# Stick-breaking attention: from cumulative sums by matmul to a sigmoid, a scan along the keys and DMA transposes, emitted by a stream scheduler

## The chip, the cores and the metric

One Trainium2 chip, all 8 cores, each with one of the 8 sequences of the batch; no core needs another. The metric is the device time of the slowest core in microseconds (us). Executions fall in a fast state or in a slower one, in which the cores of one die or of both are granted a lower TensorE clock (in the change's run of 3783.9 us 0.81 to 0.82 on cores 0 to 3, 0.92 to 0.93 on the others); only fast executions are compared here, and a range of fast runs is given where it matters. Ratios are the mean time of one kernel's fast runs over that of the other's fast runs of the same rounds on the same chip, with a 95% interval, so they are not quite the ratio of the medians quoted.

Names: PE is TensorE (matmul), PEld its weight load, DVE VectorE, ACT ScalarE, POOL GpSimd, SP SyncE, which here only starts DMAs. "L954" is line 954 of the kernel in question; experiments that add lines shift these numbers by a few.

## The reference, cut to what matters

Two layers on a (2048, 2048) sequence: an mLSTM layer with 8 heads, then a stick-breaking layer with 16 heads of width 128. Each ends with an output projection and a layer norm. The second layer's attention:

```python
# [cut] q, k, v: [B, H, S, 128], swept in blocks of 128 queries over the causal prefix
z = jnp.einsum("bhtd,bhsd->bhts", qb, kp) * scale
mask = jnp.arange(t1)[None, :] < (t0 + jnp.arange(QBLOCK))[:, None]
log_1mb = jnp.where(mask, jax.nn.log_sigmoid(-z), 0.0)
between = lax.cumsum(log_1mb, axis=3, reverse=True) - log_1mb   # sum over s<j<t
a = jnp.where(mask, jnp.exp(jax.nn.log_sigmoid(z) + between), 0.0)
outs.append(jnp.einsum("bhts,bhsd->bhtd", a, vp))
# [cut] y = (att * silu(z_gate)) @ w_out; x = LayerNorm(alpha * x + y)
```

With r(s) the product of sigmoid(-z) over the keys from s to the query, a weight is a(s) = r(s+1) - r(s). That is what the change uses: one sigmoid, one running product, one subtraction of neighbours.

## The kernel before

A small layer records every operation with the tiles it reads and writes, and places the semaphore waits, each as an instruction of its own:

```python
def _wait(self, e, dep):
    # [cut] nothing to do if e has already seen this value
    self.seen[e][sn] = v
    self.eng[e].wait_ge(self.semobj[sn], v)

def op(self, e, fn, R=(), W=(), inc=True):
    R, W = self._norm(R, W)
    self._deps(e, R, W)          # _wait for each writer of R, each writer and reader of W
    ins = fn()
    # [cut] then_inc, bookkeeping
```

Stick-breaking, keys on partitions. Per step (512 queries by 128 keys) three ACT passes and four matmuls; the projections of the next head are a generator of which each step pulls two portions of four matmuls:

```python
# s_front(k)
kb.op("pe", lambda: P_.matmul(PS[zb][:, fs], lhsT=KT[...], rhs=QT[:, qs], ...))      # QK
kb.op("act", lambda: A_.activation(out=E[i][:, fs], in_=PS[zb][:, fs], func=AF.Exp, scale=scale), ...)
kb.op("act", lambda: A_.activation(out=SP[i][:, fs], in_=E[i][:, fs], func=AF.Ln, bias=1.0, scale=1.0), ...)
# [cut] masks on POOL on the diagonal
# s_utri(k), s_tri(k): the cumulative sum along keys as two triangular matmuls
kb.op("pe", lambda: P_.matmul(PS[2][:, fs], lhsT=NUTRI[:], rhs=SP[i][:, fs], ...), ...)
kb.op("pe", lambda: P_.matmul(PS[2][:, fs], lhsT=NTRI[:], rhs=SP[i][:, fs], ...), ...)
kb.op("act", lambda: A_.activation(out=X[xi][:, fs], in_=PS[2][:, fs], func=AF.Exp), ...)
kb.op("dve", lambda: V.tensor_tensor(out=AT[ai][:, fs], in0=E[i][:, fs], in1=X[xi][:, fs], op=ALU.mult), ...)
# s_av(k)
kb.op("pe", lambda: P_.matmul(PS[3][:, fs], lhsT=VV[:, sg, :], rhs=AT[ai][:, fs], ...), ...)
# the sweep
for k in range(-2, nst + 1):
    # [cut] s_utri(k-1), s_tri(k), s_av(k-1), s_front(k+2)
    gen = pull(gen, 2)           # projections of head h+1
```

## Time and profile before

| | us |
|---|---|
| time, median of the first 3 runs | 3915.86 (3874.2 to 3988.66) |
| fastest runs in all the sessions | 3874 to 3882 |
| mLSTM layer, to the first matmul of its output layer | 1342.9 |
| stick-breaking, first projection to last AV matmul | 1625.5 to 3609.8 |
| one of its steady heads | 120 |
| its output layer, first matmul to the end | 3611.4 to 3880.5 |

The prediction below shows the page, the stages and a steady head's chain of waits.

### The profile page before, as it was taken

What the parts mean: (1) busy time and instruction counts of PE and PEld (TensorE: products, weight loads), DVE (VectorE), ACT (ScalarE), POOL (GpSimd) and SP (SyncE); (2) the same over time, 40 slices, a digit from 0 to 9 for tenths busy, and PEclk for the clock granted to TensorE, in tenths of its full rate; (3) what the DMA queues carried; (4) which work ended last, traced back from release to release, by engine and by line L of the source; (5) the groups of instructions that cost most, each with busy time, mean ns of one, the idle gap of its engine ahead of it and who ended that gap; (6) DMA issues with size and microseconds to landing.
All of it is one profiled execution on the core that took longest, in us unless ns stands there. A gap on an engine that the chain in (4) does not pass through costs nothing.

```text
span 3880.5 us, 51216 instructions; the slowest of 8 cores (3860.4 to 3880.5 us)
## 1 busy us (share of the span) xinstructions
PE 3149.9 (81%) x14916; PEld 1399.1 (36%) x14916; DVE 1532.9 (40%) x3247; ACT 1709.5 (44%) x3342; POOL 685.9 (18%) x860
## 2 busy tenths in 40 slices
PE   4889888988989499787797777977779777794887
PEld 4344444444444244333333333333333333331333
DVE  2254554454452555323333333333333333332455
ACT  2254454454453322125555555555555455555100
POOL 1121121121221022211111111111111111111122
PEclk8899999999999599899999999999899999896999
DMA  9231431331330633321112211122111221124233
GB/s 207 22 34 12 42 30 17 39 34 17 39 34 6 130 121 131 91 23 17 17 17 22 22 15 17 15 22 22 16 18 12 22 22 17 17 25 73 109 136 125
DMA packets 295422, 175.38 MB, mean 45 GB/s; under 512 B 267920, under 2 KB 284400, under 8 KB 284400
## 3 DMA queue, kind: packets, MB, share of 16 engines
q0 software_dynamic: 282768, 83.96, 20.9%
q1 hardware_dynamic: 12384, 88.14, 6.2%
q8 instruction: 130, 2.13, 0.2%
q14 instruction: 140, 1.15, 0.1%
HBM read 222.49 MB, written 33.55 MB: 66 GB/s over the span
## 4 chain that ended last, share of the span: by engine, by line
PE 59%; DVE 13%; ACT 10%; issue 9%; DMA 5%; POOL 3%; DVEq 1%; ACTq 0%; POOLq 0%; SPq 0%
PE PS L849 24%; PE PS L576 10%; PE PS L291 6%; PE PS L917 4%; PE PS L472 4%; DVE SCR L450 3%; DMA WB<-kv_w 3%; PE PS L892 2%; PE PS L927 2%; PE PS L909 2%; ACT SCR L894 2%; ACT SCR L919 2%; POOL SCR L312 2%; ACT SP L896 2%; DMA HT<-b_w_out 1%
## 5 line engine op out<-in xcount | busy, mean ns | idle before, releaser
L849 PE MATMUL PS<-HT,WB 128*128 128x512 bf16 x4096 | 996.7, 389 | 185.7 <-DMA WB<-kv_w 183.5
L921 DVE TENSOR_TENSOR AT<-SCR 128x512 bf16<-128x512 f32 (+3 forms) x640 | 391.7, 612 | 841.8 <-ACT SCR L919 805.7
L849 PEld LDWEIGHTS PS<-HT,WB 128*128 128x128 bf16 x4096 | 403.3, 99 | 667.7 <-issue 239.9
L919 ACT ACTIVATE SCR<-PS 128x512 f32<-128x512 f32 (+3 forms) x640 | 340.9, 533 | 615.4 <-PE PS L917 374.0
L576 PE MATMUL PS<-XT,GW 128*128 128x512 bf16 x2048 | 479.2, 393 | 1.2 <-ACT SCR L583 1.2
L894 ACT ACTIVATE SCR<-PS 128x512 f32<-128x512 f32 (+3 forms) x640 | 339.5, 530 | 186.8 <-PE PS L892 180.2
L896 ACT ACTIVATE SP<-SCR 128x512 bf16<-128x512 f32 (+3 forms) x640 | 361.9, 565 | 60.5 <-ACT SCR L894 2.2
L900 POOL TENSOR_TENSOR SP<-SP,MASKSB 128x128 bf16<-128x128 bf16 x256 | 109.4, 427 | 1576.8 <-ACT SP L896 1576.7
L917 PE MATMUL PS<-SP,NTRI 128*128 128x512 bf16 (+3 forms) x640 | 224.2, 350 | 121.8 <-POOL SP L900 34.7
L576 PEld LDWEIGHTS PS<-XT,GW 128*128 128x128 bf16 x2048 | 205.1, 101 | 244.5 <-issue 34.6
L927 PE MATMUL PS<-AT,VVb 128*128 128x512 bf16 (+3 forms) x640 | 226.3, 354 | 32.9 <-DVE AT L921 28.5
L291 PE MATMUL PS<-HT,XT 128*128 128x512 bf16 x1024 | 226.1, 382 | 22.9 <-DVE SCR L296 21.4
L909 PE MATMUL PS<-SP,NUTRI 128*128 128x512 bf16 (+3 forms) x576 | 199.8, 347 | 54.4 <-ACT SCR L919 53.1
L472 PE MATMUL PS<-XT,WB 128*128 128x512 bf16 x1024 | 239.9, 387 | 4.8 <-ACT DB L425 2.7
L892 PE MATMUL PS<-QTb,KTb 128*128 128x512 bf16 (+3 forms) x640 | 227.6, 356 | 0.0
L291 PE MATMUL PS<-XT,HT 128*128 128x512 bf16 x1024 | 225.6, 382 | 1.6 <-DVE HT L734 1.6
L233 PE MATMUL PS<-XT,WB 128*128 128x512 bf16 x1024 | 222.3, 379 | 0.0
L312 POOL TENSOR_TENSOR SCR<-SCR,LNG 128x2048 f32<-128x2048 f32 x32 | 144.3, 4509 | 432.7 <-DVE SCR L309 432.7
L917 PEld LDWEIGHTS PS<-SP,NTRI 128*128 128x128 bf16 x640 | 61.5, 96 | 346.5 <-issue 339.4
L811 DVE CAST KTb<-PS 128x512 bf16<-128x512 f32 x64 | 44.3, 692 | 322.4 <-PE PS L917 260.6
L594 POOL TENSOR_TENSOR SCR<-SCR 128x512 f32<-128x512 f32 x64 | 80.9, 1263 | 427.9 <-ACT SCR L592 427.9
L291 PEld LDWEIGHTS PS<-HT,XT 128*128 128x128 bf16 x1024 | 99.9, 98 | 149.0 <-issue 33.1
(150 smaller groups left out, 3287.2 us busy)
## 6 DMA issues: line engine op xcount, KB each, us to landing
y<-SCR SPq DMA_DIRECT2D x32, 1024.0 KB, 3.9
SCR<-x SPq DMA_DIRECT2D x24, 1024.0 KB, 5.8
WB<-a_w_in POOLq DMA_DIRECT2D x32, 512.0 KB, 6.3
GW<-a_w_in POOLq DMA_DIRECT2D x32, 512.0 KB, 11.4
WB<-kv_w POOLq DMA_DIRECT2D x32, 512.0 KB, 6.7
WB<-b_w_in POOLq DMA_DIRECT2D x32, 512.0 KB, 7.8
SCR<-y SPq DMA_DIRECT2D x16, 1024.0 KB, 4.8
HT<-x SPq DMA_DIRECT2D x8, 1024.0 KB, 13.1
```

The source lines that it names most:

```text
L291: kb.op("pe", lambda: P_.matmul(PS[bank][:, :], lhsT=mid[:, c, t * 128:(t + 1) * 128], rhs=wo_buf[:, c, nb * 512:(nb + 1) * 512], start=(c ...
L472: kb.op("pe", lambda: P_.matmul(PS[bank][:, :], lhsT=WB[u.slot][:, c, :], rhs=XT[:, c, tb * 512:(tb + 1) * 512], start=(c == 0), stop=(c = ...
L576: kb.op("pe", lambda: P_.matmul(PS[gb_][:, :], lhsT=gw[:, c, :], rhs=XT[:, c, tb * 512:(tb + 1) * 512], start=(c == 0), stop=(c == KC - 1) ...
L849: kb.op("pe", lambda: P_.matmul(PS[bank][:, :], lhsT=WB[u.slot][:, c, :], rhs=SRC[:, c, tb * 512:(tb + 1) * 512], start=(c == 0), stop=(c ...
L892: kb.op("pe", lambda: P_.matmul(PS[zb][:, fs], lhsT=KT[:, sg * 128:(sg + 1) * 128], rhs=QT[:, qs], start=True, stop=True), R=[kK, kQ], W=[ ...
L894: kb.op("act", lambda: A_.activation(out=E[i][:, fs], in_=PS[zb][:, fs], func=AF.Exp, scale=scale), R=[("ps", zb)], W=[f"E{i}"])
L896: kb.op("act", lambda: A_.activation(out=SP[i][:, fs], in_=E[i][:, fs], func=AF.Ln, bias=1.0, scale=1.0), R=[f"E{i}"], W=[f"SP{i}"])
L909: kb.op("pe", lambda: P_.matmul(PS[2][:, fs], lhsT=NUTRI[:], rhs=SP[i][:, fs], start=False, stop=False, skip_group_check=True), R=["NUTRI" ...
L917: kb.op("pe", lambda: P_.matmul(PS[2][:, fs], lhsT=NTRI[:], rhs=SP[i][:, fs], start=first, stop=False, skip_group_check=True), R=["NTRI", ...
L919: kb.op("act", lambda: A_.activation(out=X[xi][:, fs], in_=PS[2][:, fs], func=AF.Exp), R=[("ps", 2)], W=[f"X{xi}"])
L921: kb.op("dve", lambda: V.tensor_tensor(out=AT[ai][:, fs], in0=E[i][:, fs], in1=X[xi][:, fs], op=ALU.mult), R=[f"E{i}", f"X{xi}"], W=[f"AT{ ...
L927: kb.op("pe", lambda: P_.matmul(PS[3][:, fs], lhsT=VV[:, sg, :], rhs=AT[ai][:, fs], start=first, stop=(sg == 0), skip_group_check=True), R ...
```

## The change

Intent: take the two cumulative-sum matmuls off PE and two of three ACT passes away. Queries now lie on partitions, so that DVE's scan can run along the keys; DMA transposes bring the weights into the layout that AV needs. A scheduler orders the streams (two block slots, AV, projections, weight loads) at build time by planned durations. Weights come from the host laid out by unit of 128 columns, so that a load reads whole rows. Waits are attached to instructions where possible, and PE no longer waits for itself. The core of the diff (cut where marked):

```diff
+    LAT = {"pe": 0.25, "act": 0.12, "dve": 0.12, "pool": 0.2, "sp": 0.1}
+    def est(self, e, R, W):                     # earliest planned start
+        R, W = self._norm(R, W)                 # a PSUM bank that is read counts as written
+        t = self.t[e]
+        for k in R:
+            t = max(t, self.tw.get(k, 0.0))
+        for k in W:
+            t = max(t, self.tw.get(k, 0.0), self.tr.get(k, 0.0))
+        return t
-    def op(self, e, fn, R=(), W=(), inc=True):
+    def op(self, e, fn, R=(), W=(), inc=True, cost=0.3):
+        start = self.est(e, R, W)
         R, W = self._norm(R, W)
-        self._deps(e, R, W)
+        need = self._need(e, self._deps(R, W))  # skips PE on PE
+        attach = None
+        if e != "pe" and need:
+            attach = need.pop()
+        for sn, v in need:
+            self.eng[e].wait_ge(self.semobj[sn], v)
         ins = fn()
+        if attach is not None:
+            ins._wait_ge(self.semobj[attach[0]], attach[1])
+        self.t[e] = start + cost
+        self._time(start + cost + self.LAT[e], R, W)
# [cut] Sched.run: of all streams, emit the operation with the earliest planned start
# [cut] in phase_b, instead of s_front, s_utri, s_tri, s_av:
+            def proj():
+                for i in range(len(units)):              # per head K, Q, V, Z
+                    if kind == 0:
+                        yield lambda h=h: st["heads"] >= h - 2
# [cut] 4 x 16 matmuls of 512 columns (planned 0.216 us each), evictions
+                    if kind == 2:
+                        yield Op("sp", None, R=["VT"], W=[("VV", par)], cost=2.5,
+                                 dma=dict(slot=f"vv{par}", out=VVs[par][:], in_=VT[:], transpose=True))
+                    if kind == 3:
+                        st["proj"] = h
+                for nb in range(4):
+                    yield Op("pool", None, W=[skey], cost=11.0,
+                             dma=dict(slot=f"wo{nb}", out=SRC[:, :, nb * 512:(nb + 1) * 512], in_=b_w_out[nb]))
+            def tblock(k, slot):                         # one block of 128 queries
+                yield lambda: st["proj"] >= h
+                yield lambda: st["av"] >= 4 * h + gq - 2
# [cut] for each chunk of up to 1024 keys: QK matmuls into one of two PSUM areas, then
+                    yield Op("act", ... func=AF.Sigmoid, scale=-scale ...)
+                    yield Op("dve", ... V.tensor_tensor_scan(
+                        out=RR[slot][:, lo:hi][:, ::-1], data0=PZ[zi][:, 0:w][:, ::-1], data1=mk[:, ::-1],
+                        initial=init, op0=ALU.mult, op1=ALU.max), ...)
+                    yield Op("pool", ... G.tensor_tensor(
+                        out=AA[slot][:, b0 * 128:b1 * 128], in0=RR[slot][:, lo + 1:hi + 1], in1=RR[slot][:, lo:hi],
+                        op=ALU.subtract), ...)
+                yield Op("sp", None, R=[f"AA{slot}"], W=[("TT", gi, j)], cost=0.3 + n * 0.15,
+                         dma=dict(..., in_=AA[slot][:, 0:128 * n], transpose=True))
# [cut] AV from TT, product with the gate, result to DRAM
+            Sched(kb).run([av(), counted(0), counted(1), loads(), proj()])
```

## The prediction

The forecast's sums came to 45 us a head for DVE and 56.7 us for the slots, and that PE "stays the longest" at 70 us rested on them. The total of about 3200 us adds up from the terms that stand. Rival 4 is that the granted clock falls. The "about 14 us" for a load is an estimate; 16.4 us is the median landing of these loads before. The 93% at clock 0.99 is the slowest core's; over the eight cores PE was busy 88 to 93% of that stretch, at a clock of 0.98 to 1.00.

> **What bounds the kernel now.** I read the page first, then the per-stage table (busy time by stretch), then the chain of waits inside one steady head of the stick-breaking layer, then the list of waits. All eight cores agree (3860.4 to 3880.5 us), so this is one kernel's limit and not a slow core's. The page:
>
> ```profile
> PE 3149.9 (81%) x14916; PEld 1399.1 (36%) x14916; DVE 1532.9 (40%) x3247; ACT 1709.5 (44%) x3342; POOL 685.9 (18%) x860
> PE   4889888988989499787797777977779777794887
> PEclk8899999999999599899999999999899999896999
> ```
>
> PE leads, but not evenly: its busy digits are 8 to 9 in the first third (mLSTM and its output layer) and 7 from slice 18 on, the stick-breaking layer. The clock is no issue (9). The stages, as columns: stretch and length, then busy us of PE, PEld, DVE, ACT, POOL, then clock, DMA share, GB/s:
>
> ```profile
> 1343.00:1600.00 257.00, 238.45 (x1256) 113.96 (x1255) 144.51 (x172) 62.46 (x74) 67.68 (x15) 0.99 0.37 135
> 2050.00:2170.00 120.00, 96.43 (x428) 39.70 (x428) 39.06 (x62) 65.83 (x124) 18.06 (x36) 0.93 0.19 18
> 3480.00:3545.00 65.00, 20.90 (x66) 5.81 (x65) 11.99 (x19) 28.01 (x52) 11.15 (x18) 0.66 0.85 128
> ```
>
> The first row shows that PE can be 93% busy on all cores at clock 0.99. The second is one of 16 equal heads: 120 us. The third is the start of the last head, where nearly nothing computes and DMA is at 0.85. Inside that steady head, the chain (start, length, what):
>
> ```profile
> 2053.35 1.28 ACT L894
> 2056.24 7.16 DMA WB<-kv_w
> ...
> 2110.65 0.23 PE PS L909
> 2111.02 0.38 PE PS L917
> 2111.39 0.22 PE PS L927
> 2111.61 0.22 PE PS L892
> 2111.82 1.73 PE PS L849 x8
> ...
> 2162.06 0.43 ACT SP L896
> 2162.60 0.52 ACT SCR L919
> 2163.16 0.60 ACT SCR L894
> ```
>
> A head has three parts. About 7 us: two table loads, then a weight load that nothing hides. About 90 us: PE runs, 8 projection matmuls in 1.73 us (0.216 each) plus four attention matmuls per step, 2.9 us a step. About 17 us (2153 to 2170): projections are used up and ACT alone sets the pace with its three passes (exp, ln, exp). Work on PE is 256 x 0.216 = 55.3 us of projections, 67,584 attention columns (four products, the fourth without its last step) x 0.216/512 us = 28.5, transposes some 1.2: 85 us of 120. The last head also pays for output weights, whose loads wait for each other on POOL's queue while the mask multiplications stand behind them:
>
> ```profile
> 3480.75 17.17 DMA HT<-b_w_out
> 3498.46 16.76 DMA HT<-b_w_out
> 3515.75 15.99 DMA HT<-b_w_out
> ```
>
> [...] Before has no scan; its 128x512 and 128x128 DVE products (692 and 281 ns) give 1.07 ns an element and 144 ns fixed[...]. [...] Before has no transpose; its small loads land in 1.6 to 3.1 us, so I take 2 us fixed for each DMA. [...]
>
> **The change, part by part.** In stick-breaking, queries now lie on partitions. Per 128-query block: QK matmuls into PSUM, one ACT sigmoid in place, one DVE scan (running product with mask), one POOL subtraction of neighbours, one DMA transpose, then AV.
>
> Removed per head: the two cumulative-sum products on PE, the V transposes on PE, two of three ACT passes, the table loads (2 x 1.28 us), the masks on POOL, and 36 waits of PE on itself (0.14 us "issue" before the L917 matmuls). Four weight buffers instead of two, loaded by a stream of their own, hide the 7 us load. Work left per head, 17,408 columns in 24 chunks:
> - PE: 55.3 + 2 x 17,408 x 0.216/512 = 70.0 us.
> - ACT: sigmoid 24 x 0.17 + 17,408 x 0.833 ns (slope of 274 and 595 ns at 128 and 512 columns) = 18.5; 16 evictions x 0.58 (mLSTM's V copies) = 9.3. Sum 28.
> - DVE: [...]eight products x 0.69 (today's output product) = 5.5.[...]
> - POOL: 24 x 0.184 + 17,408 x 2.11 ns (from its f32 products, 1262 ns at 512 and 4511 at 2048) = 41.2; four DMA issues x 1.2 = 4.8. Sum 46.
> - The slots: only two blocks are in work, each with one scan buffer and one result buffer. A scan waits for the slot's subtraction, the next block's first subtraction waits until the transpose has read the buffer. Per slot chain and head: [...]subtractions 41.2, [...]48 hand-overs x 0.1 = 4.8[...].
>
> So PE at 70 us stays the longest[...]. PE's order is fixed at build time by estimated times, so it will stand at some QK and AV matmuls. Before's steady step wastes 0.3 of 2.9 us; I take 10%: 77 us a head against 120.
>
> The ends: head 0's projections (55.3) have no attention beside them, the last head's attention has no projections. There the instruction order shows the output weights again: four loads on POOL, each waiting for the last, with two small subtractions between. Three waits x about 14 us (16.4 before[...]) = 42, plus 45 us for the blocks after them: about 85. Then the merged result, which now goes through DRAM, has to be read back before the output layer can start: about 17 us (1 MB loads landed in 4 to 7 us, four to six of them queue). The output layer itself is unchanged: 265 us from 3611 to 3876.
>
> In mLSTM the unit layout of weights gains nothing directly: the chain there has PE and DVE, not DMA. Some 90 waits of PE on itself go away, and waits ride on instructions: 92 x 0.14 is about 10 us.
>
> Sum: 1618 - 10 (through mLSTM and its output layer) + 7 (first weights) + 55 + 15 x 77 + 85 + 17 + 265 + 5 = about 3200 us.
>
> **The rivals.**
> 1. The transposes become the bound. [...] Against it: [...]the scheduler's own allowance, which looks fitted to a fast transpose. I give it 4%.
> 2. The slot chain becomes the bound. [...]with contention for POOL (46 us of it, with weight-load issues that wait for PE in the same queue) heads come to about 85 to 90 us: 3320 to 3400. For it: DVE and POOL hand over in turns with only two slots.[...] I give this 25%.
> 3. PE runs nearly without gaps, 72 us a head and 75 for the last: near 3110. For it: in the output layer PE is 93% busy. 20%.
> 4. [...] Against it: the clock was 0.99 in the densest stage with all cores in it.
>
> **Range and chances.** The middle of these is 3200 us; rival 3 less some 50 us gives the low end 3060, rival 2 the high end 3400. Even 100 us a head would give 3545, clearly faster than 3916. Only rival 1 makes it slower. Faster by over 2%: 0.95; within 2%: 0.02; slower: 0.03.
>
> **What would show it.** Right: PE digits of 9 through stick-breaking, matmuls at the chain's head, a head every 75 to 80 us[...]; subtractions near 2.35 us; no table loads there; in the last head a stretch of low PE with b_w_out loads in the chain; mLSTM at 1330 to 1345 us. Wrong: transposes taking over 6 us to land or leading the waits (rival 1 or 2)[...]; PE waiting mostly for DVE at QK matmuls (rival 2); clock under 0.9 (rival 4).

## More of the kernel before

One more view is needed for what came out: the chain of waits in a stretch of the mLSTM layer (300 to 1200 us), as shares by line.

```profile
by line: PE PS L576 34.0%; issue 11.5%; PE PS L472 10.1%; DVE SCR L450 9.6%; DVE SCR L447 2.9%; DVE C L676 2.4%; DVE BST L696 2.3%; PE PS L730 2.3%; ACT HN L721 1.9%; PE PT L486 1.5%; ACT KP L656 1.4%; DVE VX L489 1.4%; DVE HT L734 1.1%; PE
```

PE lines lead, but 12.5% of the path is two lines of DVE (L447 and L450, the four dependent products and sums of the causal convolution), and 11.5% is "issue", time in which the engine waited for nothing that the profile shows. In the trace, 0.104 us (median) pass between the end of one of these DVE operations and the start of the next, which needs its result, and a block of four starts every 3.03 us.

## The result and the profile after

Both kernels are correct. After: 3502.52 us median of 5 runs (fast runs 3498.88 to 3502.52), before beside it 3978.62 us (3874.2 to 4028.94; three of these five are slow by their time, so the median is not a fast run); ratio of the fast runs 0.898 [0.891, 0.906]. So it is faster by 10%, and 100 us above the range that was predicted.

```profile
PE 2819.5 (81%) x13444; PEld 1285.7 (37%) x13444; DVE 1606.0 (46%) x2768; ACT 1084.5 (31%) x2016; POOL 923.8 (26%) x732
...
PE   5899999999999869978878877887877877832897
...
PEclk9999999999999969989999999999999999965999
```

PE's digits in stick-breaking (slices 18 to 35) are 8 and 7, not the 9 that was foretold, at a clock near before's (0.924 over the profiled core's whole run, 0.927 before). The stages, which add up (1612 + 1476 + 134 + 23 + 252 = 3497 us, and 5 us outside the span, which the prediction had too):

| stage | before | predicted | after |
|---|---|---|---|
| start to the end of head 0's projections | - | 1670 | 1612 |
| fifteen heads with projections beside them | 120 each | 77 each, 1155 | 98.4 each, 1476 |
| last head | 130 | 85 | 134 |
| reading the merged result back | - | 17 | 23 |
| output layer to the end | 269 | 265 | 252 |

The table of busy time by stretch: one steady head in two parts, and the last head. Columns: stretch and length, then busy us (and instructions) of PE, PEld, DVE, ACT, POOL, then clock, DMA share, GB/s.

```profile
2007.00:2077.00 70.00, 53.97 (x225) 21.91 (x223) 42.02 (x28) 23.77 (x35) 34.70 (x27) 0.93 0.47 85
2077.00:2107.00 30.00, 25.45 (x107) 11.10 (x107) 2.77 (x4) 2.96 (x5) 0.57 (x1) 0.89 0.33 57
3088.00:3222.00 134.00, 28.91 (x81) 8.47 (x79) 42.31 (x28) 18.32 (x25) 37.82 (x28) 0.54 0.64 99
```

For 70 us DVE and POOL work (42 and 35 us) and PE has 54 us of work; then for 30 us PE works alone on projections and the slots stand. PE's busy time in these 100 us is 79 us, where the prediction had 70 us of work. In the last head PE has 29 us of work in 134. PE's list of waits for the whole execution (waiting line, what it waited for, us in total, times, longest):

```profile
PE PSA L954 <- DVE SCR L966: 230.1, 196, 15.1
PE PSA L994 <- DMA TT<-AA: 179.8, 50, 11.5
```

Here is most of the missing time: 410 us in which PE stood at a QK matmul (L954) for a scan to release its PSUM area, or at an AV matmul (L994) for a transpose; 306 of them lie in the fifteen heads, 105 in the last one. In the heads both stand in the middle of projection matmuls that need neither:

```profile
2027.85 1.46 PE L907 MATMUL PSA<-HT,WB 128*128 128x512 bf16 x6
2032.24 0.38 PE L994 MATMUL PSA<-TT,VVb 128*128 128x512 bf16 x1 [2.94 <-DMA TT<-AA]
...
2038.08 1.24 PE L907 MATMUL PSA<-HT,WB 128*128 128x512 bf16 x5
2040.06 0.81 PE L954 MATMUL PSA<-KTb,QTb 128*128 128x512 bf16 x3 [0.73 <-DVE SCR L966]
...
2044.36 0.43 PE L954 MATMUL PSA<-KTb,QTb 128*128 128x512 bf16 x2 [0.48 <-DVE SCR L966]
2044.63 0.59 PE L907 MATMUL PSA<-HT,WB 128*128 128x512 bf16 x2
2045.47 0.59 PE L954 MATMUL PSA<-KTb,QTb 128*128 128x512 bf16 x2 [0.25 <-DVE SCR L966]
2045.90 1.46 PE L907 MATMUL PSA<-HT,WB 128*128 128x512 bf16 x6
2047.92 0.59 PE L954 MATMUL PSA<-KTb,QTb 128*128 128x512 bf16 x2 [0.56 <-DVE SCR L966]
```

Read: six projection matmuls (L907), then 2.94 us idle until the transpose for the AV matmul landed, or 0.25 to 0.73 us until a scan let the next QK in, and then two or six projections more. The order has too little projection work ahead of each such point.

Of the durations, that of the subtraction had been predicted too long. The groups of the scan and of the subtraction (count, then busy us, mean ns of one, then idle time before and what ended it):

```profile
L971 POOL TENSOR_TENSOR AA<-SCR 128x1024 bf16<-128x1024 f32 (+7 forms) x384 | 530.8, 1390 | 506.3 <-DVE SCR L966 332.2 <-DMA TT<-AA 173.4
...
L966 DVE TENSOR_TENSOR_SCAN SCR<-PSA,SCR,MK 128x1024 f32<-128x1024 f32 x128 | 298.7, 2342 | 146.2 <-POOL AA L971 76.2 <-ACT PSA L960 64.2 <-ACT VTb L921 5.5
```

The scan of 1024 columns took 2.34 us; the subtractions sum to 33.2 us a head (predicted 41.2). The transposes of the weights landed, where nothing queued before them, 2.29 us after their issue at 3 blocks and 4.33 at 16, so 1.82 us + 0.157 per block (2 us had been predicted for the fixed part; no trace of before shows a time per block). Those of one and two blocks took longer, 3.31 and 2.66 us at the least.

### The profile page after: what moved, and what is told of

It reads as the page before. It is cut to its first block, busy times and chain, and to the rows that moved or that the text cites. A ratio compares the mean times of both kernels' runs of the same rounds, so it can differ in the third digit from the quotient of the medians.

```text
span 3497.3 us, 38611 instructions; the slowest of 8 cores (3480.0 to 3497.3 us)
## 1 busy us (share of the span) xinstructions
PE 2819.5 (81%) x13444; PEld 1285.7 (37%) x13444; DVE 1606.0 (46%) x2768; ACT 1084.5 (31%) x2016; POOL 923.8 (26%) x732
## 4 chain that ended last, share of the span: by engine, by line
PE 55%; DVE 14%; DMA 14%; POOL 6%; issue 5%; ACT 4%; SPq 1%; DVEq 0%; POOLq 0%; ACTq 0%
PE PSA L907 13%; PE PSA L651 12%; PE PSA L372 9%; DVE SCR L966 9%; DMA TT<-AA 8%; PE PSA L314 6%; PE PSA L548 6%; POOL AA L971 4%; PE PSA L994 3%; PE PSA L954 2%; DMA XT<-a_w_out 2%; ACT PSA L960 2%; DMA HT<-b_w_out 2%; POOL SCR L393 1%; DMA HT<-x 1%
## 5 line engine op out<-in xcount | busy, mean ns | idle before, releaser
L971 POOL TENSOR_TENSOR AA<-SCR 128x1024 bf16<-128x1024 f32 (+7 forms) x384 | 530.8, 1390 | 506.3 <-DVE SCR L966 332.2
L907 PE MATMUL PSA<-HT,WB 128*128 128x512 bf16 x2048 | 555.7, 399 | 8.8 <-DMA WB<-kv_w 8.8
L907 PE MATMUL PSA<-HT,WBx 128*128 128x512 bf16 x2048 | 505.1, 390 | 0.0
L651 PE MATMUL PSA<-XT,GW 128*128 128x512 bf16 x2048 | 477.2, 392 | 0.0
L960 ACT ACTIVATE PSA<-PSA 128x1024 f32<-128x1024 f32 (+7 forms) x384 | 287.6, 759 | 592.4 <-PE PSA L954 590.7
L966 DVE TENSOR_TENSOR_SCAN SCR<-PSA,MK 128x128 f32<-128x128 f32 (+7 forms) x256 | 340.1, 1348 | 236.0 <-ACT PSA L960 148.6
L994 PE MATMUL PSA<-TT,VVb 128*128 128x512 bf16 (+3 forms) x640 | 248.0, 397 | 180.7 <-DMA TT<-AA 179.8
L954 PE MATMUL PSA<-KTb,QTb 128*128 128x512 bf16 (+3 forms) x640 | 195.2, 373 | 230.3 <-DVE SCR L966 230.1
L966 DVE TENSOR_TENSOR_SCAN SCR<-PSA,SCR,MK 128x1024 f32<-128x1024 f32 x128 | 298.7, 2342 | 146.2 <-POOL AA L971 76.2
L907 PEld LDWEIGHTS PSA<-HT,WB 128*128 128x128 bf16 x2048 | 205.6, 102 | 250.2 <-issue 55.3
L907 PEld LDWEIGHTS PSA<-HT,WBx 128*128 128x128 bf16 x2048 | 204.5, 100 | 252.0 <-issue 28.0
L548 PE MATMUL PSA<-XT,WB 128*128 128x512 bf16 x1024 | 235.0, 382 | 2.4 <-ACT DB L502 2.4
L372 PE MATMUL PSA<-XT,HT 128*128 128x512 bf16 x1024 | 225.4, 381 | 4.7 <-DMA XT<-a_w_out 4.7
L314 PE MATMUL PSA<-XT,WB 128*128 128x512 bf16 x1024 | 222.3, 379 | 0.0
L954 PEld LDWEIGHTS PSA<-KTb,QTb 128*128 128x128 bf16 x640 | 54.3, 99 | 360.4 <-issue 337.4
L994 PEld LDWEIGHTS PSA<-TT,VVb 128*128 128x128 bf16 x640 | 68.3, 107 | 287.4 <-issue 241.7
## 6 DMA issues: line engine op xcount, KB each, us to landing
HT<-x SPq DMA_DIRECT2D x8, 1024.0 KB, 10.3
```

Source lines behind the costliest of these rows:

```text
L314: kb.op("pe", lambda: P_.matmul(PS[bank][:, :], lhsT=WB[u.slot][:, c, :], rhs=src[:, c, tb * 512:(tb + 1) * 512], start=(c == 0), stop=(c ...
L372: kb.op("pe", lambda: P_.matmul(PS[bank][:, :], lhsT=midf(c, t), rhs=wo_buf[:, c, nb * 512:(nb + 1) * 512], start=(c == 0), stop=(c == KC ...
L548: kb.op("pe", lambda: P_.matmul(PS[bank][:, :], lhsT=WB[u.slot][:, c, :], rhs=XT[:, c, tb * 512:(tb + 1) * 512], start=(c == 0), stop=(c = ...
L651: kb.op("pe", lambda: P_.matmul(PS[gb_][:, :], lhsT=gw[:, c, :], rhs=XT[:, c, tb * 512:(tb + 1) * 512], start=(c == 0), stop=(c == KC - 1) ...
L907: yield Op("pe", lambda c=c, bank=bank, i=i, tsl=tsl: P_.matmul(PS[bank], lhsT=WS[i % 4][:, c, :], rhs=SRC[:, c, tsl], start=(c == 0), sto ...
L954: yield Op("pe", lambda zi=zi, o=o, ww=ww, b0=b0: P_.matmul(PZ[zi][:, o:o + ww], lhsT=QTs[par][:, tb * 128:(tb + 1) * 128], rhs=KTs[par][: ...
```

## The experiments

A number "per head" below is the mean over heads 2 to 14 of one trace: the time from the end of one head's last output product to the same of the next, PE's idle time just before its QK and its AV matmuls in it, and PE's busy time in it; "clock" is the TensorE clock granted over these heads. The experiments ran on several chips; the change itself was not run again beside them, but before was, and its fastest run was 3874 to 3880 us on each. The theories (O' is O once its cause was found; "in the second place" means behind the opened gate): **G**, blocks of the next head may not start until all four of its projections are emitted; **S**, two slots with one buffer each are too few; **T**, the transposes hold things back; **O**, the order built from planned durations makes PE stand; **L**, the serialised loads make the last head; **W**, attached waits made the mLSTM layer faster.

| kernel | fast runs, us | head | before QK | before AV | PE busy | clock |
|---|---|---|---|---|---|---|
| the change | 3499 to 3503 | 98.4 | 10.3 | 9.9 | 78.2 | 0.935 |
| gate_kq | 3322 to 3323 | 89.9 | 11.2 | 4.0 | 74.7 | 0.966 |
| third_slot | 3406 to 3410 | 93.5 | 9.2 | 8.8 | 75.5 | 0.947 |
| two_results | 3419 to 3421 | 95.6 | 12.2 | 8.3 | 75.1 | 0.973 |
| plain_copies | 3410 | 92.2 | 10.2 | 6.8 | 75.2 | 0.970 |
| costs_only | 3540 to 3543 | 102.5 | 10.3 | 13.6 | 78.6 | 0.928 |
| gate_costs | 3417 to 3421 | 95.6 | 12.3 | 7.0 | 76.2 | 0.946 |
| gate_two | 3361 to 3363 | 92.1 | 12.6 | 4.5 | 75.0 | 0.963 |
| gate_third | 3324 to 3334 | 90.9 | 10.4 | 4.9 | 74.9 | 0.967 |
| pe_latency | 3316 to 3320 | 87.5 | 8.8 | 4.4 | 74.0 | 0.927 |
| pe_latency_gate_costs | 3265 to 3273 | 86.1 | 1.1 | 9.5 | 75.4 | 0.939 |
| pe_latency_gate_two | 3127 | 77.7 | 2.1 | 2.9 | 72.7 | 0.961 |

A head is PE's busy time plus its standing, and both move. In two_results PE stands no less than in the change (20.5 against 20.3 us a head); its gain is 3.1 us of busy time, at a clock of 0.973 against 0.935. In pe_latency the busy time falls by 4.2 us although the clock is lower (0.927), with 6.2 stops of PE a head (idle times over 0.06 us) instead of 15.5. So the clock alone does not explain the busy time; clock and stops both may have a part in it, and no run separates them. In standing alone the gate is worth 5.0 us a head, the third slot 2.3, plain copies 3.3 and pe_latency 6.8.

### gate_kq

```diff
-                yield lambda: st["proj"] >= h
+                yield lambda: st["qk"] >= h          # set after kind == 1; av() now waits for st["proj"] >= h
```

> One line of the changed kernel's scheduling is altered: score blocks of a head may be emitted as soon as that head's K and Q projections are emitted (before: only after all four projections, K, Q, V and Z); the AV products still wait for all four. Theory G (the gate: a head is about 70 us of slot work followed by about 30 us in which the PE projects alone because the next head's blocks may not start): a head falls from 98-100 us to 80-86 us, the fifteen heads save 200 to 290 us, total 3210 to 3300 us, and the idle stretches of the DVE of about 19 us per head are gone. Theory T (the DMA transposes hold the slots and AV back) and theory S (two slots and one result buffer each are too few): the 30 us stretch is only moved into longer waits, heads stay at 93 us or more, total 3400 to 3500 us.

Measured: 3322.98 us median, ratio 0.855 [0.850, 0.861]; heads 89.9 us, the last head 80 us from the last projection to the last AV matmul (134 in the change). The gate is real, but a head is 4 to 10 us longer than theory G had it, the total lies above its range, and PE still stands for the scans nearly as often:

```profile
PE PSA L957 <- DVE SCR L969: 208.1, 165, 9.7
PE PSA L998 <- DMA TT<-AA: 77.5, 32, 16.7
```

The AV waits fell to less than half, the QK waits only from 230 to 208 us.

### third_slot

```diff
-            RR = SCR
+            RR = SCR + [sa("RR2", [128, 2056], F32)]      # and a third AA; blocks k = slot, slot+3, ...
```

> A third slot is added: a third score row buffer and a third result buffer, blocks handed out in turn over three chains. Theory S (a slot's chain of sigmoid, scan, subtraction, transposition is what the head's 70 us consist of, two are too few): heads fall to 80-88 us, total 3200 to 3320 us. Theory G: the stretch in which the slots may work is shortened from 70 us towards the PE's own need in it, but the 30 us of projections alone stay; heads 90-97 us, total 3380 to 3490 us. Theory T: 3450 us or more.

Measured: 3407.82 us, heads 93.5 us, as theory G had it for the heads; theory S's 80 to 88 did not come.

### two_results

```diff
-            AA = [sa(f"AA{i}", [128, S], BF16) for i in range(2)]
+            AA = [sa(f"AA{i}", [128, S], BF16) for i in range(4)]   # block k uses AA[k % 4]
```

> Each slot gets two result buffers, so that the subtraction of the slot's next block does not wait for the transposition of its last one (POOL waits 173 us for it in all, 76 times). Theory S: the slot's chain is shortened by 2 to 4 us a block, heads 85-92 us, total 3270 to 3380 us. Theory G: the wait is on one slot while the other works, at most 4 us a head, total 3440 to 3500 us. Theory T: 150 to 200 us less, as this wait is a wait for transposes.

Measured: 3420.48 us median, ratio 0.880. The subtraction's waits for transposes are gone from the ten longest of POOL's list, but the head lost only 2.8 us, and PE stood no less in it; a larger part came off the last head, which was 38 us shorter by its last output product. None of the three stated ranges holds exactly.

### plain_copies

```diff
-   out=TT[gi][:, 0:n, j * 128:(j + 1) * 128], in_=AA[slot][:, 0:128 * n], transpose=True
+   out=<TT[gi], flat>[:, j * 2048:j * 2048 + 128 * n], in_=AA[slot][:, 0:128 * n]        # wrong result on purpose
```

> Wrong result on purpose: the 256 transposing transfers of the score blocks become plain contiguous copies of the same bytes from the same buffer into the same tile (zeroed once before, so that nothing unwritten is read); the waits and the AV products keep their places. The V transposes stay. Theory T (transposes are the missing time): at least 150 us less, total 3200 to 3350 us, heads 80-88 us. Theories G and S: the transposes land in 2.3 to 4.3 us where nothing queues before them, so at most 4 us a head are saved: total 3430 to 3500 us.

Measured: 3410.39 us, heads 92.2 us: 92 us less in all, more than theories G and S allowed and less than T asked. So the transposes matter a little, but the same holds for each of four unrelated relaxations: each makes the head 3 to 9 us shorter and leaves PE with 9 to 12 us of QK waits. That suggests something common to all of them, and the order is a candidate.

### costs_only, gate_costs

```diff
-                        op=ALU.subtract), ..., cost=0.15 + w * 0.0022)
+                        op=ALU.subtract), ..., cost=0.175 + w * 0.001675)
-        self.tdma = max(self.tdma, start) + cost                # one DMA queue for all in the plan
+        self.tdq[q] = max(self.tdq.get(q, 0.0), start) + cost   # [cut] transposes: 1.3 us of SP, landing 1.9 + 0.157 n
```

> Only the durations with which the stream scheduler orders the instructions are altered, to what the trace shows: a subtraction 0.175 us + 1.675 ns per column (it had 0.15 + 2.2), weight loads no longer hold back the transposes in the model (it had one DMA queue for all), a transpose holds the issuing engine 1.3 us (the one of V 5.8) and lands after 1.9 us + 0.157 us per block, matmuls at 0.93 of full speed. No wait, buffer or gate changes. Theory O (the PE stands because the order was built with wrong durations): heads fall from 98 us by 8 us or more, total 3300 to 3400 us. Theories G and S: the order is good enough, the gates and buffers set the head: within 40 us of the changed kernel, 3460 to 3540 us.

> The opened gate (3323 us, heads 90 us) with the corrected durations of the scheduler. Theory O in the second place (once the gate is open, what is left is order): heads 80-85 us, total 3200 to 3270 us. Theory S in the second place (buffers): 3300 to 3350 us.

Measured: 3540 us and 3419 us, heads 102.5 and 95.6 us. Both are slower than the same kernel with the old durations, by 4 and 6 us a head (the first at the upper edge of what theories G and S allowed, the second above both ranges). So the order does matter, but truer durations made it worse: a sign that a larger error of the plan had been met halfway by the smaller ones.

### gate_two, gate_third

The edits of gate_kq and of two_results, or of third_slot, together.

> The opened gate with two result buffers a slot. Alone the gate took 8.5 us from a head and the second result buffer 2.8 us. If they shorten different stretches (theory S in the second place) the head is 86-87 us and the total 3230 to 3280 us, the last head keeps its gain of 37 us; if the same stretch, within 15 us of the opened gate alone, 3305 to 3335 us.

> The opened gate with a third slot. Alone they took 8.5 and 4.9 us from a head. Theory S in the second place: the sum, heads 83-86 us, total 3210 to 3270 us. Theory O in the second place (the PE's order is what leaves it standing, more slots do not help): heads 88-90 us, 3290 to 3330 us.

Measured: heads 92.1 and 90.9 us against 89.9 for the gate alone; gate_two's 3361 us is even above the range for no gain, and why it is 38 us slower than the gate alone was not looked into. Once the gate is open, more buffers and a third slot bring nothing under this order, and theory S falls for it.

### pe_latency: the plan's error

Printing the plan itself (its own numbers, not the chip's) gave heads of 120.7 us, with 50 us of PE "waiting" in front of projection matmuls. The reason is in the code: after each operation the plan marks the written tile as ready 0.25 us later (LAT of PE), and the next matmul of the same accumulation writes the same PSUM bank, so it "waits" for that. The plan has 0.466 us between projection matmuls; the chip runs them 0.216 us apart (3.24 us for 15 in the chain of waits). A static order that spreads QK and AV evenly over a PE at half its pace puts half the projections needed before each of them.

```diff
-        self._time(start + cost + self.LAT[e], R, W)
+        self._time(start + cost + (self.LAT[e] if inc else 0.0), R, W)   # only the last of a group
```

> One line of the scheduler's bookkeeping: a matmul within an accumulation no longer makes the next matmul into the same bank wait 0.25 us in the plan (only the last of a group does). The trace has the projections' matmuls 0.23 us apart, the plan has 0.47, so the changed kernel plans 119 us of PE for a head's projections that take 59, and puts each QK after half as many projections as would fill its wait. Theory O' (the PE stands at QK and AV because the plan has the PE at half its pace): the 20 us of PE idle time a head (10.3 before QK, 9.9 before AV) fall to 10 or less, the head to 84-89 us, total 3280 to 3360 us, without opening the gate. Theory G: the gate leaves the slots idle whatever the order; heads 95-99 us, total 3440 to 3510 us.

Measured: fast runs 3315.77 and 3319.87 us, ratio 0.856 [0.854, 0.858]; heads 87.5 us, PE idle 13.5 us a head instead of 20.3 (theory O' asked for 10 or less), with the gate closed as before. The order, in the view of PE's timeline:

```profile
2010.22 7.50 PE L907 MATMUL PSA<-HT,WBx 128*128 128x512 bf16 x34
2017.56 0.92 PE L954 MATMUL PSA<-KTb,QTb 128*128 128x512 bf16 x4
2018.31 3.83 PE L907 MATMUL PSA<-HT,WBx 128*128 128x512 bf16 x17
2021.98 2.43 PE L994 MATMUL PSA<-TT,VVb 128*128 128x512 bf16 x12
2024.25 0.81 PE L907 MATMUL PSA<-HT,WBx 128*128 128x512 bf16 x3
2024.90 0.97 PE L954 MATMUL PSA<-KTb,QTb 128*128 128x512 bf16 x4
2025.71 5.77 PE L907 MATMUL PSA<-HT,WBx 128*128 128x512 bf16 x26
```

34, 17 and 26 projections now stand between the groups of QK and AV, with no idle time before these, where the change had 2 to 14. The waits:

```profile
PE PSA L954 <- DVE SCR L966: 196.6, 61, 13.7
PE PSA L994 <- DMA TT<-AA: 91.5, 32, 10.9
```

Where the QK waits had come 196 times, they come 61 times; the 197 us that are left are longer ones (up to 13.7 us), where projections have run out.

### pe_latency_gate_costs, pe_latency_gate_two

The repaired plan with the opened gate, and either the corrected durations or two result buffers a slot with the old durations.

> The plan without the false PE latency, the opened gate, and the corrected durations together. Alone the corrected durations made the head 4 us longer and with the gate 6 us longer, which theory O' reads as a plan made wronger in one place while it is wrong by a factor of two in another. Theory O': with the plan right the PE is nearly always busy, heads 77-82 us (75 us of matmuls and a few of waits), total 3140 to 3220 us. Rival (durations on the chip scatter too much for any static order, or the buffers bind): heads 86 us or more, total above 3270 us.

> The plan without the false PE latency, the opened gate, and two result buffers a slot, with the old durations. Without the plan's repair the second buffer added nothing to the gate (92 against 90 us a head). Theory O': heads 78-84 us, total 3150 to 3240 us, as slack in buffers now counts. Rival (the order is not it): 88 us or more, above 3300 us.

Measured: heads 86.1 us with the corrected durations (3267.51 us median, ratio 0.843 [0.842, 0.844]), at the edge of what the rival claimed and not the 77 to 82 that theory O' asked for: with one result buffer, AV matmuls stand 9.5 us a head for transposes. With two result buffers heads are 77.7 us and the one fast run took 3127.36 us (the other three slow; the same kernel is run again below). PE's waits and the page of that kernel:

```profile
PE PSA L958 <- DVE SCR L970: 72.1, 27, 9.3
PE PSA L999 <- DMA TT<-AA: 50.0, 17, 7.0
```

```profile
PE 2735.2 (88%) x13444; PEld 1284.8 (41%) x13444; DVE 1608.1 (51%) x2768; ACT 1078.8 (35%) x2016; POOL 925.7 (30%) x732
...
PE   5799999999999996799699999999999999954997
...
PEclk8899999999999997899899999999999999976998
```

The 410 us of standing have become 122, the digits of the heads are 9. A steady head in the table by stretch:

```profile
2004.00:2082.00 78.00, 72.83 (x336) 32.63 (x335) 44.80 (x32) 26.73 (x40) 35.05 (x29) 0.96 0.60 98
```

336 matmuls in 72.8 us of 78: near the 70 us of work and 7 of standing that the prediction had. The second buffer brought nothing behind the gate under the wrong order; under the right one it or the gate is worth having: the repaired plan with the gate alone and with the buffer alone were not run, so how the last 9.8 us (87.5 to 77.7) divide between them stays open, as does whether the corrected durations would help beside two buffers.

### wo_keys: the last head

```diff
-                    yield Op("pool", None, W=[skey], cost=11.0,
+                    yield Op("pool", None, W=[skey] if nb == 0 else [("WO", nb)], cost=3.0,
```

The chain of waits of the change, at its last head:

```profile
3088.80 17.53 DMA HT<-b_w_out
...
3106.99 17.75 DMA HT<-b_w_out
...
3125.38 18.96 DMA HT<-b_w_out
...
3147.61 3.54 POOL AA L971 x2
```

Three loads of the output weights end to end, then POOL gets to its subtractions.

> In the changed kernel the four loads of the output weights no longer wait for one another: only the first waits for the last projection, the other three follow it in the same queue. Theory L (POOL's queue stands at these loads, so the last head's subtractions stand behind them): the last head falls from 134-147 us to 90-110 us, total 3450 to 3475 us, the other heads unchanged at 98 us. Rival (the last head is bound by its own slots' chain, the loads only show in the chain of waits): under 10 us less.

The edit also plans 3 us for each load instead of 11. Measured: fast runs 3476.03 to 3476.78 us, 26 us less and just above theory L's range; the heads stay at 98.6 us; from the last projection matmul to the last AV matmul 110 us instead of 134. The loads leave the chain of waits. Theory L names half of the last head's miss; what is left is a chain of single hand-overs (scans, and transposes of 8.3 and 13.0 us while the loads are in flight), with 25 us of "issue" between them that the profile does not explain.

### best_a, best_a_again, gate_two_again

All that helped, and its twin without the edit of wo_keys. (The last head's 84 us in the first expectation is counted from the last output product of the head before it; the 94 and 99 us below are counted from the last projection.)

> All parts that helped, together: the plan without the false PE latency, the opened gate, two result buffers a slot, and the loads of the output weights that do not wait for one another. Against the run without the last part (fast run 3127 us, heads 77.7, last head 84): theory L: the last head 70-80 us, total 3105 to 3130 us. If the loads are by now hidden: 3120 to 3145 us. In both cases faster than before by 19 per cent or more and than the change by 10 or more.

> The combination once more: 3105 to 3180 us in fast runs, by the clock that the chip grants; on cores with a clock near 0.94 a span near 3110 us. If the loads' waits still matter, 10 to 25 us under the twin without that part; if they are hidden by the repaired plan, within 8 us of it.

> The same without the change of the output weights' loads: 3120 to 3190 us in fast runs, near 3123 us on cores with a clock of 0.94.

best_a itself fell on a chip whose cores 0 and 1 had a clock of 0.917 and 0.915 and spans of 3182 and 3190 us, while its core 2 at 0.942 took 3110.5; its fast runs, 3172 to 3216 us, tell little. On one chip, five rounds each: best_a_again 3135.74 to 3140.36 us, ratio 0.8097 [0.8083, 0.8111]; gate_two_again 3128.64 to 3133.14 us, ratio 0.8079 [0.8059, 0.8098]. So the loads' waits no longer cost anything in this combination (the last head is 94 us without the edit and 99 with it), and the best version is pe_latency_gate_two: 19% under before and, by 3131 against 3502 us, 11% under the change.

### no_attach, before_attach, no_attach_look: the mLSTM layer

The change with every wait as an instruction again (`if False and need:` in place of `if e != "pe" and need:`), and the kernel before with attached waits alone (its `_wait` collects into a dictionary, `op` attaches the last).

> The changed kernel with every wait as an instruction of its own again (none attached to the instruction that needs it); the order and the dropped waits of PE on itself stay. Theory W (the attached waits gave most of the 64 us in the mLSTM layer): the layer before the first stick-breaking projection ends 45 to 65 us later, the stick-breaking heads gain 1 to 3 us each, total 3560 to 3620 us. Rival (the dropped waits of PE on itself, or the weight layout, gave it): at most 15 us later there, total 3500 to 3540 us.

> The kernel before with one part of the change alone: on all engines but PE the last wait of an instruction is attached to it and no longer an instruction of its own. Theory W: the mLSTM layer, up to the start of its output layer, takes 45 to 65 us less than the 1343 us of before; with the old stick-breaking layer's waits, which lie mostly on the PE's path, 20 to 60 us more may be gained: total ratio 0.972 to 0.988. Rival (weight layout or PE's waits on itself): at most 15 us less in the mLSTM layer, ratio 0.993 to 1.0.

> The same kernel as no_attach, for a profile in the fast state. Theory W: the output layer of the mLSTM layer starts 45 to 65 us later than in the changed kernel (1275 us), near 1330; a stick-breaking head takes 101-104 us. Rival: it starts before 1290 us.

Measured: no_attach's fast runs are 3610.11 to 3625.17 us. no_attach_look, fast: 3613.4 us, the output layer of the mLSTM layer starts at 1348.8 us (1274.7 in the change), and a head takes 99.8 us (98.4 in the change), below the 101 to 104 that were expected. before_attach: 3776.66 to 3782.68 us, ratio 0.974 [0.972, 0.976], and that output layer starts at 1287.4 us (1342.9 before). So attaching waits is worth 55 us there in the kernel before and 74 in the change (the 74 from one execution with a mean clock of 0.913 to 0.918 against 0.922 to 0.926, which may have its part in them); without it the change starts that output layer 6 us later than before did, although PE's waits on itself and the old weight layout are gone. The chain of waits, 300 to 1200 us, in before_attach and then in no_attach_look:

```profile
by line: PE PS L587 37.7%; PE PS L244 20.6%; PE PS L483 16.6%; PE PS L741 3.2%; issue 2.4%; PE PT L497 1.8%; DVE SCR L461 1.5%; DVE VX L500 1.4%; DVE STM L662 1.2%; PE PS L677 1.0%; DVE SS L717 0.9%; ACT HN L732 0.9%; POOL SCR L605 0.9%; PE
```

```profile
by line: PE PSA L651 35.3%; PE PSA L548 11.8%; issue 10.5%; DVE SCR L526 9.6%; DVE SCR L523 3.0%; PE PSA L804 2.6%; DVE C L750 2.0%; PE PSA L562 2.0%; DVE BST L770 1.9%; ACT HN L795 1.7%; DVE VX L565 1.4%; ACT KP L730 1.2%; DVE STM L725 1.2
```

With attached waits PE's projection lines hold 75% of the path, the convolution on DVE has left it but for 1.5%, and "issue" is 2.4%; without them the list is that of the kernel before. The gap between two dependent convolution operations is 0.104 us (median) in the kernel before and 0.035 us in the change, and a block of four starts every 3.03 and 2.83 us; in no_attach_look's chain it is 3.03 us again (621.30 to 624.33). So in the change, where PE's projection lines hold the path (75%) as in before_attach, a block of four on DVE is 7% shorter; the same edit attached waits on ACT and POOL too, so that DVE alone did it is not shown.

## Why the prediction was right or wrong

- **Direction, and the durations off PE:** right. The fixed part of the transposes' landing (1.82 us against 2), ACT (27.1 against 28) and DVE (44.8 against a sum of 45) held; the scans took 39.9 us a head, by their means at 128 and 512 columns (407 and 1211 ns) 2.09 ns a column, where before's products took 1.07; the subtractions were over-estimated by 8 us (33.2 against 41.2), off the path. DVE and POOL worked side by side without a loss that shows: a subtraction of 1024 columns took 1.89 us with a scan beside it for over 80% of its time (31 cases), and 1.89 us with one for under 5% of it (63 cases).
- **"PE stays the longest ... it will stand at some QK and AV matmuls ... I take 10%: 77 us a head":** this step failed, and it alone puts the time out of the range: a head took 98.4 us, and 15 x 21.4 us are 321 us. The larger term is the standing, 20.3 us a head instead of 7. The 10% was carried over from before, whose order is a hand-made interleave; the new order is made from a plan, and the plan's durations were not compared with the trace, though both were at hand: 0.216 us between projection matmuls in the chain of waits of before, and 0.216 + 0.25 in the new bookkeeping. pe_latency shows it by itself (10.9 us a head, 6.8 of them standing). The second part, the gate on all four projections, stood in the diff too and was not seen (8.5 us a head by itself, 5.0 of them standing). With both put right and a second result buffer, a head takes 77.7 us. The smaller term is PE's own work, 78.2 us busy instead of 70.0. The prediction priced 512 columns at 0.216 us throughout; the same sum gave it 85 us for a head of before, where its own table shows 96.43 us busy at a clock of 0.93. In the repaired kernel the matmuls of a head take 72.7 us, so 5.5 of the 8.2 us came with the stops of the order or with the clock (0.935 against 0.961).
- **Rival 1 (transposes the bound):** wrong: 0.157 us a block were measured, so the 136 blocks of a head add 21.4 us. **Rival 2 (slots bound, 85 to 90 us):** its sum was wrong, its time nearer than the main line's. Slots and buffers added nothing behind the open gate under that order. The sign named for it, "PE waiting mostly for DVE at QK matmuls", did appear, and came from order: the same sign has two causes. **Rival 3:** reached in a form by the repaired kernel, 3127. **Rival 4:** not in the change (mean clock 0.92 to 0.93 on all cores).
- **The last head, 85:** mis-sized, 134. The chain of three loads was foretold with 42 us and took 54; the 45 us for the blocks behind it became some 78 (3144.3 to 3222): less than the prediction's own 56.7 us for a head of slots had been allowed for them. wo_keys shows 24 us of it to be the loads.
- **mLSTM, 10 us:** mis-sized, 68 us by the start of its output layer. The prediction named PE and DVE as the chain there, but counted only PE's waits on itself (92 x 0.14 us, which is 13 and not 10); between DVE's dependent operations 0.104 us became 0.035, 0.07 us for each attached wait.
- **Read-back 17, output layer 265:** 23 and 252; the latter was 268 us in the run without attached waits, so these give that gain too. These 13 us and the 58 of the mLSTM layer were not foreseen and hid part of the miss: without that luck the time would have been near 3570 us.

## What to carry to other kernels

When an order is made at build time from a plan, print the plan and compare its pace with the trace: improving single durations can make the order worse while a larger error stands. When work is priced from durations, sum the kernel before in the same way and compare with its busy time: here 85 us against 96 would have shown the price to be too low. An engine that waits for buffers in the middle of work that needs none may have too little of that work ahead of the wait; before adding buffers, look at how much stands between the waits. Attached waits are worth looking for where a chain of short dependent operations runs on one engine (0.07 us at each step here), and they may change which engine sets the time.

## Further prices that the runs show

- The weights' transposes, SBUF to SBUF: in transfers of 3 to 16 blocks each further block of 128x128 (32 KB) cost 157 ns, which is 209 GB/s, with 1.8 us fixed; a transfer of one block landed 3.3 us after its issue at the least. The issue held SP for 1.1 to 1.6 us (medians, up to 14 blocks).
- The transposes of V, also 16 blocks, write a contiguous buffer and were not faster. The one that had no 512 KB weight load in flight beside it landed after 4.6 us (4.3 for the weights' 16 blocks); the fifteen that had one held SP for some 5.8 us and landed after 7.7 to 9.3 us, and the weights' transposes of 15 blocks that had one were as late (7.5 us or more, 4.2 without). No run here changed the loads alone.
- A wait as an instruction of its own against one attached: 0.104 against 0.035 us between dependent DVE operations, 108 to 123 us of 3500 in this kernel (fast runs of no_attach against 3502).
- POOL's subtraction of f32 neighbours into bf16: 1.89 us for 1024 columns, faster for its length than its f32 products here (1.26 us for 512).
